# Queries on the un-normalized residual: five of sixteen query slabs of a product-key expert layer, and the row products beside them

## The chip, the cores and the metric

One core of one Trainium2 chip. The time is device microseconds of one execution of the whole program, from first to last instruction with what lies around them; several executions make a median. Lower is better.

The engines are PE (TensorE, matrix products; PEld is its weight load), DVE (VectorE), ACT (ScalarE), POOL (GpSimd) and SP, whose queue issues most DMAs. Each runs its own instructions in order and waits on semaphores for the others.

## The reference, cut to what matters

256 tokens of 1024 features pass through a first block (modulation, mixer, experts) and then two layers of a second block. The part in question is the seam between the mixer's output and the experts' queries:

```python
x = x + g1[:, None, :] * rms_norm(y, norm1_post[l])
h = modulate(rms_norm(x, norm2_pre[l]), sh2, sc2)      # h * (1 + sc2) + sh2
y = peer(h, peer_wq[l], ...)

def peer(h, wq, subkeys, u, v):
    q = (ht @ wq).reshape(T, P_HEADS, 2, P_DKH)         # 16 slabs of 128 columns
    s = jnp.einsum('thcd,hcnd->thcn', q, subkeys)       # scores, then top-k
    ...                                                 # experts u and v
```

The deviation of rms_norm is one number for each token. So with `A = norm2_pre * (1 + sc2)` and `B = sh2` for each feature and `r` for each token, `h @ wq = r * ((x * A) @ wq) + B @ wq`: `r` can go onto the product's result, and `B @ wq` is one number for each query column.

The second block's modulation is a matrix product of one row: `mod = silu(c2) @ mod_w + mod_b`, 6 x 1024 numbers for each of its layers. It needs nothing of the tokens, so it can be computed anywhere before its use.

## The kernel before, in words

All activations lie transposed: features on the 128 partitions, 8 chunks of 128 features by 256 tokens. A product in fp32 is three matmuls (`mm3`, L402-406): both operands are split into a rounded high half and the remainder, and high x high, high x low and low x high are added in PSUM. Weights come in slabs of 128 output columns (512 KB) into five raw buffers; `warm` (L308-325) splits a slab ahead of its use, the high half on ACT (L315), the low half on DVE (L323). `block` (L408) runs one slab: 8 chunks x 3 products. `blocks` (L424) runs several slabs chunk by chunk, so that each chunk of the input is used by all of them as soon as it is there. What follows a slab's products is a generator: `spawn` queues it, and `advance("pre")` and `advance("post")` in each later block take it one step further. The order of instructions on each engine is the order in which this Python code issues them; no scheduler changes it.

The seam before, in the order of issue (L1082-1159):

- w_out, 8 slabs. Each result is scaled into `y` (L1082) and squared on ACT; sums over tokens' features are products with a column of ones (`colstat`, L567).
- `resid_rms` (L660): the deviation (`rstd` L581: one DVE step, a power on POOL), its broadcast over the partitions by PE (`bcast2`, L576), then chunk by chunk `y` x deviation (L671), the residual's addition (L674), the square of the new `x` on ACT (L1104), the second norm's sums on PE.
- `peer` (L1129-1141): the second deviation and its broadcast, then `x` x deviation on DVE (L1137), `* A + B` on ACT (`affine`, L681), the high half on ACT (L683) and the low half on DVE (L400).
- The copy of `x` to memory (`xd`, L1145) and the load of the subkeys (`sub`, L1391), both issued by POOL.
- `blocks` of query slabs 0 to 2, then `block` for slabs 3 to 15. Each slab's result is copied by ACT (L1418), multiplied by the subkeys on PE (L1422), and sorted on DVE by a side generator (`topk`).

Both norms are chains on DVE, ACT and POOL. Beside them PE runs the class `Rows` (L227-265): the first 8 units of 128 columns of `mod`, as products of a single weight column with 512-column pieces of the weight's rows, 32 matmuls that show as 64 records. `PAUSES` says how many of them stand at which of the seam's places, and the rest stand behind the second broadcast (L1146). The result is a row, which ACT copies out of PSUM (L259) and POOL sends through memory to become columns (L261, L262).

The other units of `mod` are row dots on DVE (`dot`, L519-523), one unit for each 512 KB load and instruction of 128x1024 (L522). They are spread over other stages: `RATES[0]` is how many of them stand beside each block of the v stage (784 to 1140 us), from its sixth block to its 123rd.

Of the kernel before, what the change touches and what calls it, by code (L numbers as in the profile page):

```python
# [11 lines left out]
F32 = mybir.dt.float32  # L12
F32R = mybir.dt.float32r
# [15 lines left out]
RATES = [0.54, 0.0, 0.45, 0.4, 0.5, 0.15]  # L29
# [16 lines left out]
ROW_UNITS = 8  # L46
PAUSES = [3, 2, 2, 2, 2, 2, 2, 1, 0, 3, 3]
# [3 lines left out]
OFF, HALF = 4, 8  # L51
EPS = 1e-6
# [6 lines left out]
SPANS = (slice(0, 1), slice(1, 2), slice(2, 4), slice(4, 6), slice(6, 8))  # L59
# [70 lines left out]
def _rowsN(w):  # L130

    return np.ascontiguousarray(w.reshape(-1, P, w.shape[1]))
# [13 lines left out]
def _layout(i):  # L146
    o = {}
# [26 lines left out]
    o["mod0r"] = _rowsN(np.ascontiguousarray(i["mod_w_2"][0][:, :ROW_UNITS * P]))  # L174
# [7 lines left out]
    m = i["mla_w_in_2"][0]  # L182
# [4 lines left out]
    r = uq[:, :, 128:]  # L187
# [39 lines left out]
class Rows:  # L227


    def __init__(self, body, name, c8, place, depth):  # L230
        self.b, self.w, self.c8, self.place, self.depth = body, body.a[name], c8, place, depth
        self.raws, self.at, self.ps = [], 0, None
        self.load(depth)

    def load(self, n):
        while len(self.raws) < min(n, KC):
            raw = self.place()
            self.b.nc.sync.dma_start(raw, self.w[len(self.raws)])
            self.raws.append(raw)

    def step(self, n):

        if self.ps is None:
            self.ps = [self.b.pst() for _ in range(2)]
        for _ in range(min(n, 4 * KC - self.at)):
            kc, q = divmod(self.at, 4)
            self.b.nc.tensor.matmul(self.ps[q // 2][0:1, (q % 2) * T:(q % 2 + 1) * T], self.c8[:, kc:kc + 1],
                                    self.raws[kc][:, q * T:(q + 1) * T], start=kc == 0 and q % 2 == 0, stop=kc == KC - 1,
                                    skip_group_check=True)
            self.at += 1  # L250
            if q == 3:
                self.load(kc + 1 + self.depth)

    def finish(self, dst, bias, scr):

        nc = self.b.nc
        self.step(4 * KC)
        for n in range(2):
            nc.scalar.activation(scr[:, n * 512:(n + 1) * 512], self.ps[n][0:1], AF.Copy)  # L259
        line = self.b.dr.tile([1, D], F32, name="line")  # L260
        nc.gpsimd.dma_start(line, scr)  # L261
        nc.gpsimd.dma_start(dst, line.rearrange("o (k p) -> p (o k)", p=P))  # L262
        yield "post"
        yield "post"
        nc.vector.tensor_tensor(dst, dst, bias, ALU.add)


class Body:
# [391 lines left out]
    def resid_rms(self, st, y, dst, scr, then, idle=lambda n: None):  # L660

        nc = self.nc
        r = self.rstd(st, 2, EPS, D)
        self.warm()
        idle(0)
        bc = self.bcast2(r)
        for n in range(len(SPANS) + 1):
            idle(n + 1)
            if n < len(SPANS):
                s = SPANS[n]  # L670
                nc.vector.tensor_tensor(scr[:, s], y[:, s], self.wide(bc, s), ALU.mult)  # L671
            if n > 0:
                s = SPANS[n - 1]
                nc.vector.tensor_tensor(dst[:, s], scr[:, s], self.x[:, s], ALU.add)  # L674
                then(s)

# [44 lines left out]
    def mixer(self):  # L721
        nc, a = self.nc, self.a
        with ExitStack() as ctx:
            self.tmps = ctx.enter_context(self.pool_l("tmps1", 14))
            sp = ctx.enter_context(self.pool_l("mix", 1))
            self.mctx = ExitStack()
            mp = self.mctx.enter_context(self.pool_r("mraw", 4))
# [3 lines left out]
            x = self.x  # L731

            c8 = self.cp.tile([P, KC], F32, name="c8")
# [331 lines left out]
            self.prate = 0.0  # L1065
            c82 = self.cp.tile([P, KC], F32, name="c82")
            nc.scalar.activation(c82, self.colr("c2", 0, KC), AF.Sigmoid)
            nc.vector.tensor_tensor(c82, c82, self.colr("c2", 0, KC), ALU.mult)
            rows = self.rows = Rows(self, "mod0r", c82, lambda: mp.tile([P, D], F32, name="mraw"), 4)
# [23 lines left out]
            self.drain()  # L1093
            for j in range(8):
                if j == 7:
                    self.warm()
                self.block("w_out", j, mixa, g_y(j))
            self.drain()
            st2 = self.st2 = self.pst()

            wait = []

            def then(s):
                nc.scalar.activation(sgm[:, s], x[:, s], AF.Square)  # L1104
                if wait:
                    w = wait.pop()
                    nc.vector.tensor_tensor(sgm[:, w.start], sgm[:, w.start], sgm[:, w.start + 1], ALU.add)
                    self.colstat(st2, sgm[:, w.start], 0, False)
                if s.start in (2, 4):
                    wait.append(s)  # L1110
                else:
                    for j in range(s.start, s.stop):
                        self.colstat(st2, sgm[:, j], 0, j == 0)
            self.resid_rms(st, y, x, sga, then, lambda n: rows.step(PAUSES[1 + n]))


    def peer(self):
        tc, nc, a = self.tc, self.nc, self.a
        NB = 88
        with ExitStack() as ctx:  # L1120
# [8 lines left out]
            r = self.rstd(self.st2, 2, EPS, D)  # L1129
            self.rows.step(PAUSES[9])  # L1130
            bc = self.bcast2(r)
            self.rows.step(PAUSES[10])
            a2 = self.scale_cols("a2", self.colr("norm2_pre", 0, 8), self.ada[:, 32:40])
            self.warm()
            low = None
            for s in SPANS:
                nc.vector.tensor_tensor(za[:, s], self.x[:, s], self.wide(bc, s), ALU.mult)  # L1137
                if low:
                    low()
                low = self.affine(za, a2, self.ada[:, 24:32], h, s, za[:, 8 + s.start:10 + s.start])  # L1140
# [5 lines left out]
            self.rows.step(4 * KC)  # L1146
            self.mctx.close()
            self.xctx.close()
            tctx = ExitStack()
            tp = tctx.enter_context(self.pool_r("topk", 1))  # L1150
# [4 lines left out]
            self.blocks([("wq", b) for b in range(3)], h, [g_q(b) for b in range(3)], tail=3)  # L1155
            self.spawn(self.rows.finish(self.mod[0][:, 0:8], self.colr("mod_b", 0, 8), za[0:1, 20:24].rearrange("p a t -> p (a t)")))
            self.side, self.side_rate = side, 1.4
            for b in range(3, 16):
                self.block("wq", b, h, g_q(b))
# [227 lines left out]
    def topk(self, tp, t2, iota, iT, ss):  # L1387
# [27 lines left out]
        def g_q(b):  # L1415
            def gen(pq):
                q = t2.tile([P, T], F32, name="q")
                nc.scalar.activation(q, pq[:, :T], AF.Copy)  # L1418
# [664 lines left out]
```

## Time and profile before

| | |
|---|---|
| median of 3 runs | 1738.02 us (1731.5 to 1740.38) |
| profiled execution | 1743.28 us |
| its span | 1741.4 us |
| PE busy | 1707.6 us (98%) |
| DVE busy | 1382.3 us (79%) |
| ACT busy | 1038.1 us (60%) |
| POOL busy | 215.7 us (12%) |
| mean granted clock of PE | 0.992 |

The profile is of one execution, the times are of three others. Busy shares are means over stages. A row of a timeline gives the start, the duration, the engine, the line of the kernel, what is written and read, how many instructions the row holds, and in brackets how long the engine was idle before and what released it. PE's matmuls overlap: the distance of two starts, not the duration, is what one costs. [...]

### The profile page before, as it was taken

How to read it: one execution, taken by the hardware profiler on the slowest of the kernel's cores; microseconds unless marked ns; L12 is line 12 of the kernel's file. 1: busy time of each engine (PE TensorE's matmuls, PEld its weight loads, DVE VectorE, ACT ScalarE, POOL GpSimd, SP SyncE). 2: the span in 40 equal slices, each digit the busy share in tenths (PEclk: the TensorE clock that was granted, in tenths of full speed). 3: DMA queues.
4: the chain of work that ended last, by engine and by line, in shares of the span. 5: the costliest groups of instructions: out<-in, count | busy, mean ns of one | idle time of the engine just before them, and what ended most of it. 6: DMA issues, size and time to landing. Idle time of an engine off the chain costs nothing.

```text
span 1741.4 us, 33346 instructions
## 1 busy us (share of the span) xinstructions
PE 1707.6 (98%) x12720; PEld 1595.9 (92%) x12720; DVE 1382.3 (79%) x2845; ACT 1038.1 (60%) x1912; POOL 215.7 (12%) x236
## 2 busy tenths in 40 slices
PE   8999999999999999999999999999999999999997
PEld 4899999799999999998888888889999998999997
DVE  3788778679988889997888888876899867688754
ACT  3764444455554999985555555556675457567543
POOL 1110000000010775540000000030200000020001
PEclk8999999999999999999999999999999999999999
DMA  7676677545555454447898888853467665446552
GB/s 271 244 262 214 232 246 248 206 158 178 187 193 183 160 166 161 158 167 251 295 328 301 293 296 308 282 190 123 130 241 279 246 239 169 147 133 206 183 184 70
DMA packets 102400, 371.17 MB, mean 213 GB/s; under 512 B 11456, under 2 KB 11968, under 8 KB 101856
## 3 DMA queue, kind: packets, MB, share of 16 engines
q1 hardware_dynamic: 101664, 365.76, 61.8%
q0 software_dynamic: 576, 3.29, 0.5%
q8 instruction: 99, 1.62, 0.4%
q14 instruction: 61, 0.50, 0.1%
HBM read 365.99 MB, written 2.10 MB: 211 GB/s over the span
## 4 chain that ended last, share of the span: by engine, by line
PE 91%; DVE 4%; ACT 3%; issue 1%; POOL 1%; DMA 0%; POOLq 0%; ACTq 0%; DVEq 0%
PE ps L404 20%; PE ps L406 19%; PE ps L405 19%; PE ps L1282 6%; PE ps L1281 6%; PE ps L1283 6%; PE ps L1210 2%; PE ps L571 1%; PE ps L451 1%; PE ps L452 1%; PE ps L453 1%; PE ps L746 1%; PE ps L476 1%; PE ps L478 1%; PE ps L477 1%
## 5 line engine op out<-in xcount | busy, mean ns | idle before, releaser
L315 ACT ACTIVATE whi<-wraw 128x1024 fp32r<-128x1024 f32 (+1 forms) x548 | 573.8, 1050 | 447.2 <-PE ps L405 194.2
L323 DVE TENSOR_TENSOR wlo<-wraw,whi 128x1024 fp32r<-128x1024 f32 (+1 forms) x538 | 650.5, 1213 | 52.7 <-ACT whi L315 51.4
L404 PE MATMUL ps<-h2h,whi 128*128 128x256 f32 x1152 | 329.8, 286 | 0.0
L406 PE MATMUL ps<-h2h,wlo 128*128 128x256 f32 x1152 | 320.3, 278 | 0.6 <-DVE wlo L323 0.6
L405 PE MATMUL ps<-h2l,whi 128*128 128x256 f32 x1152 | 317.4, 276 | 0.0
L406 PE MATMUL ps<-hhh,wlo 128*128 128x256 f32 x800 | 225.2, 281 | 4.2 <-DVE wlo L323 4.2
L404 PE MATMUL ps<-hhh,whi 128*128 128x256 f32 x800 | 228.1, 285 | 0.8 <-ACT hhh L683 0.8
L405 PE MATMUL ps<-hhl,whi 128*128 128x256 f32 x800 | 224.9, 281 | 1.3 <-DVE hhl L400 1.1
L404 PEld LDWEIGHTS ps<-h2h,whi 128*128 128x128 f32 x1152 | 216.4, 188 | 0.4 <-ACT za L681 0.4
L405 PEld LDWEIGHTS ps<-h2l,whi 128*128 128x128 f32 x1152 | 216.7, 188 | 0.0
L406 PEld LDWEIGHTS ps<-h2h,wlo 128*128 128x128 f32 x1152 | 215.5, 187 | 0.9 <-DVE wlo L323 0.8
L1282 PE MATMUL ps<-whi,al 128*128 128x512 f32 x512 | 199.5, 390 | 0.8 <-DVE al L400 0.8
L1281 PE MATMUL ps<-whi,ah 128*128 128x512 f32 x512 | 199.2, 389 | 0.0
L1283 PE MATMUL ps<-wlo,ah 128*128 128x512 f32 x512 | 199.2, 389 | 0.0
L1202 POOL TENSOR_SCALAR L<-iota,i1T,eT 128x128 bf16<-128x128 f32 x128 | 141.0, 1108 | 272.3 <-DVE mT L1504 137.0
L522 DVE SCALAR_TENSOR_TENSOR mraw<-mraw,crow 128x1024 f32<-128x1024 f32 x128 | 157.2, 1228 | 0.0
L406 PEld LDWEIGHTS ps<-hhh,wlo 128*128 128x128 f32 x800 | 150.9, 189 | 4.8 <-DVE wlo L323 4.8
L404 PEld LDWEIGHTS ps<-hhh,whi 128*128 128x128 f32 x800 | 152.1, 190 | 2.4 <-ACT hhh L683 1.6
L405 PEld LDWEIGHTS ps<-hhl,whi 128*128 128x128 f32 x800 | 151.2, 189 | 2.7 <-DVE hhl L400 2.4
L404 PE MATMUL ps<-hh,whi 128*128 128x256 f32 (+1 forms) x440 | 126.0, 286 | 0.7 <-ACT hh L683 0.7
L406 PE MATMUL ps<-hh,wlo 128*128 128x256 f32 (+1 forms) x440 | 123.2, 280 | 0.5 <-DVE wlo L323 0.5
L405 PE MATMUL ps<-hl,whi 128*128 128x256 f32 (+1 forms) x440 | 122.9, 279 | 0.2 <-DVE hl L400 0.2
(463 smaller groups left out, 3511.4 us busy)
## 6 DMA issues: line engine op xcount, KB each, us to landing
wraw<-u SPq DMA_DIRECT2D x128, 512.0 KB, 3.3
wraw<-v SPq DMA_DIRECT2D x128, 512.0 KB, 5.4
mraw<-mod SPq DMA_DIRECT2D x88, 512.0 KB, 3.9
wraw<-fa SPq DMA_DIRECT2D x44, 512.0 KB, 4.2
wraw<-fb SPq DMA_DIRECT2D x44, 512.0 KB, 4.1
mraw<-w_ada SPq DMA_DIRECT2D x40, 512.0 KB, 4.2
wraw<-fo SPq DMA_DIRECT2D x32, 512.0 KB, 4.4
wraw<-wq SPq DMA_DIRECT2D x16, 512.0 KB, 3.8
```

Source lines behind the costliest of these rows:

```text
L315: nc.scalar.activation(t[:, :hi - lo], self.raws[self.n_hi][:, :hi - lo], AF.Copy)
L323: e.tensor_tensor(t[:, :n], self.raws[self.n_lo][:, :n], self.his[self.n_lo].bitcast(F32)[:, :n], ALU.subtract)
L404: mm(out, lh, rh, start=start, stop=False, **kw)
L405: mm(out, lh, rl, start=False, stop=False, **kw)
L406: mm(out, ll, rh, start=False, stop=stop, **kw)
L451: mm(pts[tt][hf], ah, wh[:, s], start=kc == 0, stop=False)
L522: nc.vector.scalar_tensor_tensor(raw, raw, 1.0, self.crow, op0=ALU.mult, op1=ALU.mult, accum_out=acc)
L1202: nc.gpsimd.tensor_scalar(L[:, k], iota, i1, e, op0=ALU.is_equal, op1=ALU.mult)
L1210: nc.tensor.matmul(pg[:, k * P:(k + 1) * P], L[:, k], half[:, k, h], start=h == 1, stop=h == 0)
L1281: mm(o, ah, w[0][:, s], start=first, stop=False)
L1282: mm(o, al, w[0][:, s], start=False, stop=False)
L1283: mm(o, ah, w[1][:, s], start=False, stop=last)
```

## The change: what it does

- The residual's chunks go into query products without the second deviation. For each chunk, ACT makes the high half of `x * A` (`pre`), DVE the low half, and PE multiplies it with slabs 0, 1 and 2 at once (`prods`), beside the sums of squares. Two further columns of `pre` hold `B`, so that each product has 258 columns and the last two give `B @ wq`.
- Slabs 3 and 4 follow on the same `pre`. Behind the third chunk of slab 3 stands the second broadcast. For slabs 3 and 4 the split weights lie in spare buffers (`w4h`, `w4l`) over a tile that is free by then.
- Then `h2` is made from `x` for slabs 5 to 15: ACT copies the broadcast to SBUF (`br`), and for each chunk DVE computes `x * A * br`, ACT adds `B` and rounds, DVE makes the low half. Between the chunks stand the splits of the weights of slabs 5 to 7.
- The results of slabs 0 to 4 (`g_ql`): DVE copies the two last columns, multiplies by `br`, ACT adds `B @ wq`; then the subkeys' products as before. The side generator of the sort starts four slabs later.
- The additions of pairs of squares move from DVE to POOL. `A` and `B` are prepared during the mixer's products rather than between the norms.
- `ROW_UNITS` is 4 rather than 8: 16 row matmuls rather than 32, from two loads of 1 MB rather than eight of 512 KB. 4 of them stand before the first norm's sums, 12 between the sums and the first broadcast. The other four units become row dots on DVE: 132 rather than 128. `RATES[0]` goes from 0.54 to 0.58.

The core of the diff:

```diff
-RATES = [0.54, 0.0, 0.45, 0.4, 0.5, 0.15]
+RATES = [0.58, 0.0, 0.45, 0.4, 0.5, 0.15]
...
-ROW_UNITS = 8
-PAUSES = [3, 2, 2, 2, 2, 2, 2, 1, 0, 3, 3]
+ROW_UNITS = 4
+PAUSES = [4, 12]
...
             self.drain()
-            st2 = self.st2 = self.pst()
-
+            r = self.rstd(st, 2, EPS, D)
+            self.warm(5, 5)
+            rows.step(PAUSES[1])
+            self.spawn(rows.finish(self.mod[0][:, 0:4], self.colr("mod_b", 0, 4)))
+            self.advance("post")
+            bc = self.bcast2(r)
+            ws = [self.use(("wq", b, 0, D)) for b in range(3)]
...
+            def prods(k, b):
+                s = slice(k * P, (k + 1) * P)
+                self.mm3(qs[b][:, :T + 2], ws[b][0][:, s], ws[b][1][:, s], pre[0][:, k], pre[1][:, k], k == 0, k == KC - 1)
+
+            def high(s):
+                js = range(s.start, s.stop)
+                square = lambda: nc.scalar.activation(sgm[:, s], x[:, s], AF.Square)
+                if s.stop == KC:
+                    square()
+                for j in js:
+                    nc.scalar.activation(pre[0][:, j, :T], x[:, j], AF.Copy, scale=a2[:, j:j + 1])
+                if s.stop < KC:
+                    square()
+
+            def low(s):
+                js = range(s.start, s.stop)
+                for j in js:
+                    nc.vector.scalar_tensor_tensor(pre[1][:, j, :T], x[:, j], a2[:, j:j + 1], pre[0].bitcast(F32)[:, j, :T],
+                                                   op0=ALU.mult, op1=ALU.subtract)
                 if wait:
                     w = wait.pop()
-                    nc.vector.tensor_tensor(sgm[:, w.start], sgm[:, w.start], sgm[:, w.start + 1], ALU.add)
+                    nc.gpsimd.tensor_tensor(sgm[:, w.start], sgm[:, w.start], sgm[:, w.start + 1], ALU.add)
...
+                for j in js:
+                    for b in range(3):
+                        prods(j, b)
...
+            r = self.rstd(st2, 2, EPS, D)
+            self.warm(4, -9)
+            for b in (3, 4):
+                ws.append(self.use(("wq", b, 0, D)))
+                qs.append(self.pst())
+                for k in range(KC):
+                    prods(k, b)
+                    if b == 3 and k == 2:
+                        self.br = self.bcast2(r)
...
-            for s in SPANS:
-                nc.vector.tensor_tensor(za[:, s], self.x[:, s], self.wide(bc, s), ALU.mult)
+            for j in range(KC):
+                t = self.tmp("nx")
+                nc.vector.scalar_tensor_tensor(t, self.x[:, j], a2[:, j:j + 1], br, op0=ALU.mult, op1=ALU.mult)
+                nc.scalar.activation(h[0][:, j], t, AF.Identity, bias=b2[:, j:j + 1])
                 if low:
                     low()
...
+                if j in (1, 3, 5):
+                    self.warm(1 + j // 2, 1 + j // 2)
             low()
...
+            def g_ql(b):
+
+                pt = self.lead_q[b]
+                w = self.sm.tile([P, 2], F32, name="wq")
+                nc.vector.tensor_copy(w, pt[:, T:T + 2])
+                q = qlp.tile([P, T], F32, name="ql")
+                nc.vector.tensor_tensor(q, pt[:, :T], br, ALU.mult)
+                nc.scalar.activation(q, q, AF.Identity, bias=w[:, 0:1])
+                for _ in range(b // 2):
+                    yield "pre"
+                yield from g_q(b, q)(None)
+            for b in range(5):
+                self.spawn(g_ql(b))
+            self.advance("post")
+            self.blocks([("wq", b) for b in (5, 6)], h, [g_q(b) for b in (5, 6)])
```

How the order of instructions moves, at three places. First PE between w_out and the first query products. In the kernel before, where L247 is a row product, L571 a sum with the column of ones, L576 a broadcast, `mxh` w_out's input and `sgm` the squares:

```order
L406 MATMUL ps<-mxh,wlo 128x256
L247 MATMUL ps<-mraw,c_3186 1x256 x3
L571 MATMUL ps<-ones,ysum 128x1 x2
L571 MATMUL ps<-ones,t_ysq 128x1 x2
L247 MATMUL ps<-mraw,c_3186 1x256 x2
L576 MATMUL ps<-ident,rr 128x128 x2
L247 MATMUL ps<-mraw,c_3186 1x256 x4
L571 MATMUL ps<-ones,sgm 128x1 x2
```

From there on row products stand between all the sums, and the last 13 of them between the second broadcast and the first product of `h2h`. In the changed kernel (L244 the row product, L566 the sum, L571 the broadcast, `prqh` and `prql` the halves of `pre`, `rwhm` and `rwvs` the two 1 MB loads):

```order
L401 MATMUL ps<-mxh,wlo 128x256
L244 MATMUL ps<-rwhm,c_3190 1x256 x4
L566 MATMUL ps<-ones,ysum 128x1 x2
L566 MATMUL ps<-ones,t_ysq 128x1 x2
L244 MATMUL ps<-rwhm,c_3190 1x256 x4
L244 MATMUL ps<-rwvs,c_3190 1x256 x8
L571 MATMUL ps<-ident,rr 128x128 x2
L566 MATMUL ps<-ones,sgm 128x1 x2
L399 MATMUL ps<-prqh,whi 128x258
L400 MATMUL ps<-prql,whi 128x258
L401 MATMUL ps<-prqh,wlo 128x258
```

All row products stand ahead of the first broadcast, and query products follow behind the first sum of the new squares.

Second, PE at the end of slab 4 in the changed kernel (`sub` the subkeys, `ql` a query of `g_ql`, `h2h` and `h2l` the halves of h2):

```order
L401 MATMUL ps<-prqh,w4l 128x258
L1474 MATMUL ps<-sub,ql 128x128 x4
L399 MATMUL ps<-h2h,whi 128x256
L400 MATMUL ps<-h2l,whi 128x256
L401 MATMUL ps<-h2h,wlo 128x256
```

The subkey products of slabs 0 and 1 stand ahead of the first product on h2.

Third, DVE behind the second deviation. In the kernel before:

```order
L588 TENSOR_SCALAR rv<-ps 128x2
L648 SCALAR_TENSOR_TENSOR a_3874<-ada,cols 128x8
L1137 TENSOR_TENSOR za<-x,ps 128x256 x2
L400 TENSOR_TENSOR h2l<-za,h2h 128x256
L1137 TENSOR_TENSOR za<-x,ps 128x512
```

In the changed kernel, the end of the h2 chunks (L318 is the weight split, L1171 `x * A * br`, L1175 the low half) and the first result of `g_ql`:

```order
L318 TENSOR_TENSOR wlo<-wraw,whi 128x1024
L1171 SCALAR_TENSOR_TENSOR t_nx<-x,a_3197,i1T 128x256
L1175 SCALAR_TENSOR_TENSOR h2l<-t_nx,ada,h2h 128x256
L1171 SCALAR_TENSOR_TENSOR t_nx<-x,a_3197,i1T 128x256
L1175 SCALAR_TENSOR_TENSOR h2l<-t_nx,ada,h2h 128x256 x2
L1197 COPY wq<-ps 128x2
L1199 TENSOR_TENSOR ql<-ps,i1T 128x256
```

Each chunk of h2 takes two instructions of DVE with 256 columns, and the results of slabs 0 to 4 are taken up only behind the last chunk.

## Rows read from the trace of the kernel before

**Rows 1.** page, part 4: chain that ended last, by engine

```profile
PE 91%; DVE 4%; ACT 3%; issue 1%; POOL 1%; DMA 0%; POOLq 0%; ACTq 0%; DVEq 0%
```

**Rows 2.** windows: stretch, us, each engine's busy us (instructions), PEclk, DMA share, GB/s

```profile
322.00:344.00 22.00, 21.91 (x120) 11.46 (x119) 13.75 (x30) 10.12 (x20) 4.00 (x37) 1.00 0.59 204
```

**Rows 3.** PE's timeline, 318 to 368 us: start, us, instructions, [idle before, releaser]

```profile
322.74 0.28 PE L406 MATMUL ps<-mxh,wlo 128*128 128x256 f32 x1
...
326.59 0.71 PE L576 MATMUL ps<-ident,rr 128*128 128x128 f32 x4
...
337.41 5.77 PE L247 MATMUL ps<-mraw,c 128*1 128x256 f32 x26
343.11 0.39 PE L404 MATMUL ps<-h2h,whi 128*128 128x256 f32 x1
...
351.70 0.28 PE L404 MATMUL ps<-h2h,whi 128*128 128x256 f32 x1
...
354.69 1.85 PE L1422 MATMUL ps<-sub,q 128*128 128x128 f32 x12
...
367.05 0.38 PE L406 MATMUL ps<-h2h,wlo 128*128 128x256 f32 x1 [0.60 <-DVE wlo L323]
```

**Rows 4.** VectorE's timeline, 322 to 362 us

```profile
327.34 0.75 DVE L671 TENSOR_TENSOR sga<-y,ps 128x256 f32<-128x256 f32 x2 [0.23 <-PE ps L576]
328.01 0.42 DVE L674 TENSOR_TENSOR x<-sga,x 128x256 f32<-128x256 f32 x1
...
350.75 3.50 DVE L323 TENSOR_TENSOR wlo<-wraw,whi 128x1024 fp32r<-128x1024 f32 x3 [4.80 <-ACT whi L315]
```

**Rows 5.** ScalarE's timeline, 322 to 362 us

```profile
328.46 0.42 ACT L1104 ACTIVATE sgm<-x 128x256 f32<-128x256 f32 x1 [2.61 <-DVE x L674]
...
349.66 3.18 ACT L315 ACTIVATE whi<-wraw 128x1024 fp32r<-128x1024 f32 x3 [4.44 <-PE ps L405]
```

**Rows 6.** POOL's timeline, 322 to 362 us

```profile
336.58 0.76 POOL L1145 DMA_DIRECT2D xd<-x  x1
```

**Rows 7.** timeline of all engines, 1226 to 1230 us, VectorE and POOL

```profile
1227.08 0.74 POOL L1733 TENSOR_TENSOR t_zp<-z 128x256 f32<-128x256 f32 x1 [54.60 <-DVE z L1617]
1227.12 0.98 DVE L1625 SCALAR_TENSOR_TENSOR prel<-z,lnAB,preh 128x256 fp32r<-128x256 f32 x1 [0.19 <-ACT preh L1622]
...
1228.02 0.47 DVE L1617 SCALAR_TENSOR_TENSOR z<-ps,mod,x 128x256 f32<-128x256 f32 x1
...
1228.42 0.47 DVE L1625 SCALAR_TENSOR_TENSOR prel<-z,lnAB,preh 128x256 fp32r<-128x256 f32 x1
```

**Rows 8.** DMA issues, 300 to 365 us: KB each, median us to landing

```profile
xd<-x POOLq DMA_DIRECT2D x1, 1024.0 KB, 9.3
sub<-subk POOLq DMA_DIRECT2D x1, 1024.0 KB, 10.9
```

**Rows 9.** PE's timeline and windows around two gaps of 1.70 us

```profile
1569.19 0.39 PE L406 MATMUL ps<-hhh,wlo 128*128 128x256 f32 x1 [1.70 <-DVE wlo L323]
...
1570.03 0.42 PE L406 MATMUL ps<-hhh,wlo 128*128 128x256 f32 x1
...
1573.24 0.35 PE L406 MATMUL ps<-hhh,wlo 128*128 128x256 f32 x1
...
1571.00:1572.00 1.00, 1.00 (x7) 1.00 (x7) 1.00 (x2) 1.00 (x2) 0.00 (x0) 0.50 0.83 324
...
1267.48 0.38 PE L406 MATMUL ps<-hhh,wlo 128*128 128x256 f32 x1 [1.70 <-DVE wlo L323]
...
1268.00:1272.00 4.00, 4.00 (x36) 4.00 (x36) 3.94 (x8) 3.50 (x7) 0.00 (x0) 1.00 0.61 186
```

**Rows 10.** v stage: a window, waits for v, group of row dots

```profile
960.00:1050.00 90.00, 90.00 (x398) 74.47 (x398) 79.02 (x141) 51.28 (x79) 0.00 (x0) 1.00 0.87 297
...
ACT whi L315 <- DMA wraw<-v: 3.8, 2, 2.2
...
L522 DVE SCALAR_TENSOR_TENSOR mraw<-mraw,crow 128x1024 f32<-128x1024 f32 x128 | 157.2, 1228 | 0.0
```

More of the change, by code (lines that the diff above doesn't have):

```diff
@@ L227, with __init__ @@
 class Rows:
[L230 to L239, printed above, removed]
+    def __init__(self, body, name, c8, raws):
+        self.b, self.c8, self.raws = body, c8, raws
+        self.at, self.ps = 0, None
+        for n, raw in enumerate(raws):
+            body.nc.sync.dma_start(raw, body.a[name][n])
@@ L241, in step @@
     def step(self, n):
         if self.ps is None:
[L244 to L249, printed above, removed]
+            self.ps = self.b.pst()
@@ L250, in step, with finish @@
+        for _ in range(min(n, 2 * KC - self.at)):
+            kc, q = divmod(self.at, 2)
+            o = (kc % 4) * 2 * T + q * T
+            self.b.nc.tensor.matmul(self.ps[0:1, q * T:(q + 1) * T], self.c8[:, kc:kc + 1], self.raws[kc // 4][:, o:o + T],
+                                    start=self.at == 0, stop=kc == KC - 1, skip_group_check=True)
             self.at += 1
-            if q == 3:
-                self.load(kc + 1 + self.depth)
-    def finish(self, dst, bias, scr):
+    def finish(self, dst, bias):
@@ L262, in finish @@
         nc.gpsimd.dma_start(dst, line.rearrange("o (k p) -> p (o k)", p=P))
-        yield "post"
-        yield "post"
+        for _ in range(3):
+            yield "post"
         nc.vector.tensor_tensor(dst, dst, bias, ALU.add)
@@ L658, in wide @@
         return ap.unsqueeze(1).broadcast_to([P, s.stop - s.start, T])
[L660 to L675, printed above, removed]
     def affine(self, x, A, B, act, s, scr):
@@ L1068, in mixer @@
             nc.vector.tensor_tensor(c82, c82, self.colr("c2", 0, KC), ALU.mult)
-            rows = self.rows = Rows(self, "mod0r", c82, lambda: mp.tile([P, D], F32, name="mraw"), 4)
+            rows = Rows(self, "mod0r", c82, [sp.tile([P, 2 * D], F32, name="rw" + t, tag=t) for t in ("hm", "vs")])
+            a2 = self.a2 = self.scale_cols("a2", self.colr("norm2_pre", 0, 8), self.ada[:, 32:40])
+            pre = tuple(qp.tile([P, KC, T + 16], F32R, name="prq" + m)[:, :, o:o + T + 2] for m, o in (("h", 12), ("l", 4)))
+            b2 = self.cp.tile([P, KC, 2], F32, name="b2")
+            for n in range(2):
+                nc.vector.tensor_copy(b2[:, :, n], self.ada[:, 24:32])
+            self.split(b2, pre[0][:, :, T:], pre[1][:, :, T:])
             for j in range(8):
@@ L1093, in mixer @@
             self.drain()
+            pair = [sp.tile([P, 2 * D + HALF], F32R, name="w4" + m, tag="ya" + m)[:, :2 * D].rearrange("p (a t) -> p a t", t=D) for m in "hl"]
             for j in range(8):
@@ L1111, in then @@
                 else:
-                    for j in range(s.start, s.stop):
+                    for j in js:
                         self.colstat(st2, sgm[:, j], 0, j == 0)
-            self.resid_rms(st, y, x, sga, then, lambda n: rows.step(PAUSES[1 + n]))
+                for j in js:
+                    for b in range(3):
+                        prods(j, b)
+            for n in range(len(SPANS) + 2):
+                if n < len(SPANS):
+                    s = SPANS[n]
+                    nc.vector.tensor_tensor(sga[:, s], y[:, s], self.wide(bc, s), ALU.mult)
+                if 0 < n <= len(SPANS):
+                    s = SPANS[n - 1]
+                    nc.vector.tensor_tensor(x[:, s], sga[:, s], x[:, s], ALU.add)
+                    high(s)
+                if n > 1:
+                    low(SPANS[n - 2])
+            r = self.rstd(st2, 2, EPS, D)
[7 more added lines that the diff above has]
+                        self.br = self.bcast2(r)
     def peer(self):
@@ L1145, in peer @@
             nc.gpsimd.dma_start(xd, self.x)
-            self.rows.step(4 * KC)
-            self.mctx.close()
+            self.qctx.close()
             self.xctx.close()
             tctx = ExitStack()
+            qlp = tctx.enter_context(self.pool_r("ql", 5))
             tp = tctx.enter_context(self.pool_r("topk", 1))
@@ L1154, in peer @@
             g_q = next(side)
-            self.blocks([("wq", b) for b in range(3)], h, [g_q(b) for b in range(3)], tail=3)
-            self.spawn(self.rows.finish(self.mod[0][:, 0:8], self.colr("mod_b", 0, 8), za[0:1, 20:24].rearrange("p a t -> p (a t)")))
+            def g_ql(b):
[12 more added lines that the diff above has]
+            self.blocks([("wq", b) for b in (5, 6)], h, [g_q(b) for b in (5, 6)])
             self.side, self.side_rate = side, 1.4
-            for b in range(3, 16):
+            for b in range(7, 16):
                 self.block("wq", b, h, g_q(b))
@@ L1413, in top16, with g_q, gen @@
                 nc.vector.tensor_copy(idx, u)
[L1415 to L1418, printed above, removed]
+        def g_q(b, q=None):
+            def gen(pq, q=q):
+                if q is None:
+                    q = t2.tile([P, T], F32, name="q")
+                    nc.scalar.activation(q, pq[:, :T], AF.Copy)
                 yield "pre"
```

33 lines of the change are left out of this document (19 added, 14 removed).

## The prediction

> **What bounds the kernel now.** I read the chain that ended last first: 91% of the span is PE [rows 1]. So a change of this kernel is worth what it takes from, or adds to, PE's own stream of instructions, idle time included. Second the stretch that the change rewrites, 322 to 344 us: PE is busy 21.91 of 22.00 us there at a granted clock of 1.00 [rows 2]. The reader should see that this is a full engine and not a free one: VectorE and ScalarE have room there (13.75 and 10.12 us busy), PE none. Third PE's timeline, to see with what it is full [rows 3]: between w_out's last product (322.74) and the first query product (343.11) it does almost nothing but row products, the last 26 of which start at 337.41 and fill the 5.70 us in which h2 is made. They are useful work that covers two norms one behind the other. So the question is what covers the norms when half of that work is gone.
>
> **What is taken away.** Row products fall from 64 records to 32. One costs 5.70/26 = 0.22 us [rows 3], so PE loses 32 x 0.22 = **7.0 us** of work. That is the whole gain: every other matmul stays (the query products grow from 256 to 258 columns, 1%, for 120 of them some 0.1 us, left out).
>
> **Gap a, before the first query product.** Four row steps (8 records, 1.8 us) and the four pairs of norm sums end at about 325.9, as before. Twelve steps (24 records x 0.22 = 5.3 us) carry PE to 331.2; under them lie the norm's small operations and the splitting of three slabs, three ScalarE passes of 3.18 together and three VectorE passes of 3.50 together [rows 4, 5]. Then the broadcast of the deviation ends at 331.9, and PE has nothing more. The chain behind it, from rows of the same operations: the first y x deviation starts 0.75 after the broadcast does (327.34 against 326.59 [rows 3, 4]); two of them and the residual add take 328.01 + 0.42 - 327.34 = 1.1 [rows 4]; ScalarE's high half, then its square, 0.42 each, 0.84 [rows 5]. 331.2 + 0.75 + 1.1 + 0.84 = 333.9. PE idles **2.0 us**. Longer if the semaphores between the engines add up, shorter by nothing that I can see, since the first square is what the first sum on PE waits for.
>
> **The three slabs on the residual.** 72 products at (351.70 - 343.11)/72 = 0.119 us [rows 3] are 8.6 us, the sums 3.3; VectorE's chunks come faster than PE takes them (a 128x256 step of the kind (a x scalar) - b has starts 0.40 apart [rows 7]), once the first two are through. I put 0.4 us of waiting on that start-up. The two additions that go to POOL have a price on VectorE: beside POOL's 0.74 us addition the same step took 0.98 rather than 0.47 [rows 7]. Twice 0.5 us falls where VectorE is ahead of PE, so the sum takes 0, bound 1.0. [...]
>
> **Gap b, before the first subkey product.** This is the term that decides. PE goes on with 9 products of slab 3 and the second broadcast, whose result ScalarE copies to SBUF by about 348.4 (333.9 + 8.6 + 3.3 + 0.4 = 346.2; 1.1 for nine products, 0.7 broadcast, 0.4 copy). Only then does VectorE begin to make h2, chunk by chunk: 16 steps at 0.39 us = 6.3, two weight splits in between at 1.17 = 2.3 [rows 4], a wait of about 1.2 for the high half of the last of these slabs (ScalarE takes 1.06 for one [rows 5], behind its own h2 chunk), 0.6 for two waits on ScalarE: 10.4 us, to 358.8. Behind all of it, on the same engine, stand the copy and the multiplication for the first of the five slabs (0.4); ScalarE's bias is 0.5 more; PE's next instruction is the product of that query with the subkeys, at 359.7. The order of PE has these in front of the products of slabs 5 and 6, which would have h2 chunks to work on from 349 on. PE itself is through with slab 4 at 346.2 + 48 x 0.119 + 0.6 = 352.5. Idle: **7.2 us**. Bounds: 0.335 us a step, the distance of the plain two-operand steps at 327.34 [rows 4], and no wait for the high half would leave 5.1; a price of 0.47 each, with no overlap, makes 8.5. I keep 7.2, since the trace has the same form of step at 0.40.
>
> **Small terms.** The wait of PE at 367.05 for a weight split, 0.60 [rows 3], goes: -0.6, because that slab (7) is split under gap b. The subkeys' transfer is issued behind the copy of x on POOL's queue, 0.76 us after it [rows 6]; both wait for nothing but the second deviation and go out at about 345.2 and 345.9; 10.9 us [rows 8] later, at 356.8, the subkeys have landed, 2.9 us before they are wanted. Nothing is charged; what it is if they are late, stands among the rivals. Four more 128-wide units of mod become VectorE's row dots, 1.23 us each [rows 10], and their 512 KB loads, in the v stage with 118 blocks x 0.04 = 5 pieces more than now. There VectorE is busy 79.02 of 90 us and PE 90.00 [rows 10]: 5 x 1.5 us vanish in VectorE's idle time as long as the loads behave.
>
> **The clock.** PE's granted clock was 1.00 all through this stretch because PE never stopped. Twice the trace has a gap of 1.70 us before a product. [...] A stay at the lower level: from 1570.03 to 1573.24 PE started 15 products in 3.21 us, at 0.119 each 1.79 would have done, so a drop costs 1.4 us [rows 9]. Gap b is four times longer than one that was followed by a drop, gap a a little longer: I charge both, 2 x 1.4 = **2.8 us**. [...]
>
> **The sum.** -7.0 + 2.0 + 0.4 + 7.2 - 0.6 + 2.8 = **+4.8 us**. Against the profiled execution, 1743.28, that is 1748.1; the median of the runs shown is 1738.02, 5.3 below the profiled one, and the forecast is made against it: **1742.8 us**. 0.5%, about what a measurement of this kernel can tell from no change, is 8.7 us, so the likeliest outcome is no difference that counts. The gain cannot pass 7.0 + 0.6 = 7.6 us even with both gaps gone.
>
> **Rivals.**
> - *Shorter gaps.* VectorE's steps come 0.335 apart (16 x 0.055 = 0.9), the high half is there in time (1.2), and gap a leaves the clock alone (1.4): 4.8 - 3.5 = +1.3, **1739.3**. For it: the gap of 1.70 without a drop, and ScalarE's idle time before the last split. Against: the 0.40 of [rows 7].
> - *The v stage loses its cover* (the other side). The five further 512 KB pieces come into a stretch whose DMA share is 0.87 at 297 GB/s [rows 10]. If the v slabs, which have to land in time for ScalarE's split, are pushed back by them, PE waits: 5 x 512 KB at 297 GB/s is 8.8 us, +13.6 in all, **1751.6**. It decides from the point at which the landing takes longer than the buffers hold; ScalarE waited for v slabs twice already, 3.8 us in all [rows 10], which speaks for it. Against: PE was busy 90.00 of 90 us there in spite of that.
> - *The subkeys land late.* If the copy of x (9.3) and the subkeys (10.9) [rows 8] run one behind the other and not side by side, the subkeys land at 345.9 + 20.2 = 366.1, 6.4 after the query wants them: +11.2, **1749.2**. In the kernel before nothing shows it, as the subkeys had 17 us there.
> - *The change does not do what it says*, so that PE's stream is as before: excluded, as the order of instructions shows 16 row matmuls rather than 32 and the products on the residual ahead of h2.
>
> **How the numbers follow.** Forecast 0.72, shorter gaps 0.18, v stage 0.05, subkeys 0.05. From the forecast (+4.8) another 3.9 us makes it slower by over 0.5%, which the bounds of gap b (+1.3) and the POOL additions (+1.0) with the spread of medians reach in a small part: 0.05; faster by over 0.5% needs 13.5 us, a measurement's accident: 0.02; same 0.65. Shorter gaps: same 0.16, faster 0.02. The v stage: slower 0.04, same 0.01; the subkeys the same. Together: **faster 0.04, same 0.83, slower 0.13**. The range goes from the shorter gaps less the distance of the lowest run to the median (1739.3 - 6.5 = 1733) to the v stage's price, 1752.
>
> **What would show it.** In the changed kernel's profile: 32 row records, PE idle about 2 us before the first sum of squares and about 7 us before the first subkey product, that one released by ScalarE's bias; granted clock 0.50 for some 3 us after each; no wait of PE in slab 7; the v stage as long as before. Wrong if the gap before the subkeys is under 4 us or ends with a DMA, if the clock stays at 1.00 behind both, or if the v stage is longer by more than 2 us.

## The result, and the profile of the changed kernel

The changed kernel takes 1757.68 us (median of 6 runs, 1754.27 to 1762.07) beside 1739.55 us of the kernel before on the same chip: ratio 1.0096, 95% interval 1.007 to 1.0121. A second measurement on another occasion gave 1.0093 (1.0076 to 1.0109). By these ratios it is slower by 16 to 17 us. The forecast was 1742.8 us and no difference that counts, with a range that ended at 1752: the change costs time that counts, and the measured time lies outside the range.

The two gaps of the seam came out as forecast. PE's timeline of the changed kernel, from the row products to the first subkey product; these rows answer to [rows 3]:

```profile
320.17 1.89 PE L244 MATMUL ps<-rwhm,c 128*1 128x256 f32 x8
...
324.69 3.62 PE L244 MATMUL ps<-rwvs,c 128*1 128x256 f32 x16
328.24 0.71 PE L571 MATMUL ps<-ident,rr 128*128 128x128 f32 x4
330.97 0.61 PE L566 MATMUL ps<-ones,sgm 128*128 128x1 f32 x4 [2.02 <-ACT sgm L1107]
...
345.00 0.60 PE L571 MATMUL ps<-ident,rr 128*128 128x128 f32 x4
...
357.56 2.08 PE L1474 MATMUL ps<-sub,ql 128*128 128x128 f32 x8 [7.28 <-ACT ql L1200]
```

The two gaps are 2.02 and 7.28 us, the second is released by ScalarE's bias, and the row products cost 0.22 us a record (16 in 3.55 us). Two windows behind the gaps, with the granted clock in the third column from the end:

```profile
334.00:336.00 2.00, 2.00 (x11) 2.00 (x11) 2.00 (x5) 1.50 (x4) 1.29 (x2) 0.50 0.04 1
...
358.00:360.00 2.00, 2.00 (x11) 2.00 (x11) 0.92 (x5) 1.42 (x3) 0.00 (x0) 0.50 0.05 12
```

Behind both gaps the granted clock was 0.50 (the prediction's lower level), and so it was in a second profile of the changed kernel, where products started 0.21 us apart behind each. That the first gap brought it is not shown. In a second profile of the kernel before, which has no such gap, the granted clock was 0.50 at the same place, while PE was busy throughout with the row products and a broadcast:

```profile
333.30:336.60 3.30, 3.30 (x10) 1.38 (x9) 0.64 (x2) 0.12 (x1) 2.96 (x36) 0.50 1.01 287
```

With the gap of 2.0 us the granted clock was 0.50 there in all seven profiles, without it in two of the five that have the order of the kernel before.

What the forecast had no term for is seen in the v stage. A window of it, which answers to the first row of [rows 10], and the three groups of its products:

```profile
961.40:1051.40 90.00, 90.00 (x389) 72.96 (x388) 79.78 (x145) 49.31 (x75) 0.00 (x0) 1.00 0.87 300
```

```profile
L1333 PE MATMUL ps<-whi,al 128*128 128x512 f32 x512 | 202.4, 395 | 0.8 <-DVE al L395 0.8
L1332 PE MATMUL ps<-whi,ah 128*128 128x512 f32 x512 | 202.0, 395 | 0.0
L1334 PE MATMUL ps<-wlo,ah 128*128 128x512 f32 x512 | 202.0, 394 | 0.0
```

PE is busy 90.00 of 90 us as before, the clock is 1.00 as before, it waits for nothing, and yet it did 389 products where the kernel before did 398. The mean distance of two starts over the stage, waits left out, is 0.2324 us rather than 0.2267: 1536 products x 0.0057 = 8.7 us. Busy share, waits and granted clock all look untouched; only the count in a window of fixed length tells.

Stage by stage, in us, each from the start of a kind of product to the start of the next, of two profiles of each kernel (the second ones from the runs below):

| stage | before | before, again | changed | changed, again |
|---|---|---|---|---|
| start to w_out's last product | 322.7 | 320.0 | 320.0 | 322.5 |
| to the last subkey product | 76.4 | 78.6 | 79.6 | 82.6 |
| to the first one-hot product | 170.3 | 170.3 | 171.3 | 171.3 |
| to the v stage | 217.2 | 217.2 | 217.2 | 217.2 |
| v stage, to its last product | 349.6 | 349.5 | 358.3 | 360.4 |
| to the span's end | 605.2 | 605.8 | 606.1 | 604.7 |

On the means: seam (the second row) +3.6, the stage behind it +1.0, v stage +9.8, the rest -0.2. That is 14.2 of the 16 to 17 measured, inside the interval. Most of the seam's spread within one kernel goes with the clock. PE worked 3.4 us at a granted clock of 0.50 there in the second profile of the kernel before and none in the first; 6.5 and 13.0 us in the two of the changed kernel.

### The profile page after: what moved, and what is told of

Read it like the earlier page. It is cut to its first block, busy times and chain, and to the rows that moved or that the text cites. A ratio compares the mean times of both kernels' runs of the same rounds, so it can differ in the third digit from the quotient of the medians.

```text
span 1752.5 us, 33329 instructions
## 1 busy us (share of the span) xinstructions
PE 1710.2 (98%) x12688; PEld 1596.8 (91%) x12688; DVE 1394.7 (80%) x2882; ACT 1039.3 (59%) x1917; POOL 224.3 (13%) x239
## 4 chain that ended last, share of the span: by engine, by line
PE 85%; DVE 8%; ACT 4%; issue 2%; DMA 1%; POOL 0%; ACTq 0%; DVEq 0%; SPq 0%; POOLq 0%
PE ps L399 19%; PE ps L401 19%; PE ps L400 19%; PE ps L1333 5%; PE ps L1334 5%; PE ps L1332 5%; DVE wlo L318 2%; PE ps L1261 2%; DVE mraw L517 1%; PE ps L566 1%; PE ps L724 1%; PE ps L471 1%; PE ps L473 1%; PE ps L472 1%; DMA wraw<-v 1%
## 5 line engine op out<-in xcount | busy, mean ns | idle before, releaser
L310 ACT ACTIVATE whi<-wraw 128x1024 fp32r<-128x1024 f32 x546 | 571.5, 1050 | 447.3 <-PE ps L400 181.4
L318 DVE TENSOR_TENSOR wlo<-wraw,whi 128x1024 fp32r<-128x1024 f32 (+1 forms) x536 | 648.0, 1213 | 55.9 <-ACT whi L310 54.5
L399 PE MATMUL ps<-h2h,whi 128*128 128x256 f32 x1112 | 318.6, 287 | 0.0
L401 PE MATMUL ps<-h2h,wlo 128*128 128x256 f32 x1112 | 309.7, 279 | 0.0
L400 PE MATMUL ps<-h2l,whi 128*128 128x256 f32 x1112 | 307.3, 276 | 0.0
L399 PEld LDWEIGHTS ps<-h2h,whi 128*128 128x128 f32 x1112 | 209.6, 188 | 0.0
L400 PEld LDWEIGHTS ps<-h2l,whi 128*128 128x128 f32 x1112 | 209.5, 188 | 0.0
L401 PEld LDWEIGHTS ps<-h2h,wlo 128*128 128x128 f32 x1112 | 208.4, 187 | 0.0
L1253 POOL TENSOR_SCALAR L<-iota,i1T,eT 128x128 bf16<-128x128 f32 x128 | 146.1, 1148 | 284.2 <-PE ps L401 160.5
L517 DVE SCALAR_TENSOR_TENSOR mraw<-mraw,crow 128x1024 f32<-128x1024 f32 x132 | 161.9, 1227 | 0.2 <-DMA mraw<-mod 0.2
```

The costliest lines, as they stand in the source:

```text
L310: nc.scalar.activation(t[:, :hi - lo], self.raws[self.n_hi][:, :hi - lo], AF.Copy)
L318: e.tensor_tensor(t[:, :n], self.raws[self.n_lo][:, :n], self.his[self.n_lo].bitcast(F32)[:, :n], ALU.subtract)
L399: mm(out, lh, rh, start=start, stop=False, **kw)
L400: mm(out, lh, rl, start=False, stop=False, **kw)
L401: mm(out, ll, rh, start=False, stop=stop, **kw)
L517: nc.vector.scalar_tensor_tensor(raw, raw, 1.0, self.crow, op0=ALU.mult, op1=ALU.mult, accum_out=acc)
```

## Experiments

**Theory 1**: the slower products come from placement. The change has two new small tiles in the pools that lie first in SBUF (`b2`, 64 bytes a partition; `wq`, 2 x 32). They lift the weights' raw buffers and halves by 128 bytes (the first `whi` from 41664 to 41792), while the v stage's small operand (`ah` at 184256), in a pool that the kernel puts on the right side, stays. The distance of the two was a multiple of 256 bytes (184256 - 41664 = 142592 = 557 x 256) and is 128 off it now. **Theory 2**: the five further row dots and their loads in the v stage slow PE down, my rival of the v stage.

### The kernel before, lifted by 128 bytes

```diff
         cp = self.cp
+        cp.tile([P, 32], F32, name="shift")
```

> The kernel before with one unused tile of 128 bytes a partition in the pool that lies first in SBUF; nothing else is changed. In the changed kernel two small new tiles (64 bytes each) move the weights' halves, their raw buffers and all that lies behind them on the left side up by 128 bytes, while the activations of the v stage on the right side stay where they were. Theory 1 (placement): PE's products in the v stage read two operands whose distance decides their rate. Then this kernel has the v stage of the changed kernel: starts of products 0.2324 us apart rather than 0.227, the stage 358 us rather than 349.4, and the time 7 to 12 us above the kernel before. Theory 2 (the five further pieces and their loads slow PE down in the v stage): v stage 349.4 us, time within 3 us of the kernel before.

Measured: ratio 1.0052 (1.0031 to 1.0072), v stage 359.1 us, 0.2333 us a product. 128 unused bytes cost the kernel before about 9 us by the ratio (7.3 between the medians). Its window, with 388 products:

```profile
960.00:1050.00 90.00, 90.00 (x388) 72.39 (x387) 77.05 (x136) 50.11 (x76) 0.00 (x0) 1.00 0.84 289
```

### The changed kernel with its small tiles on the other side

```diff
-            b2 = self.cp.tile([P, KC, 2], F32, name="b2")
+            b2 = qp.tile([P, KC, 2], F32, name="b2")
...
-                w = self.sm.tile([P, 2], F32, name="wq")
+                w = qlp.tile([P, 2], F32, name="wq")
```

> The changed kernel with its two small new tiles on the right side of SBUF, so that the weights and all else on the left lie at the addresses of the kernel before. Theory 1 (placement): v stage 349.4 us, 0.227 us a product, and 8 to 9 us less than the changed kernel, which leaves the +4.8 us of the prediction's sum against the kernel before, of which 3 to 4 are seen between w_out's end and the first expert slab. Theory 2 (pieces): v stage 358 us, time as the changed kernel's.

Measured: ratio to the kernel before 1.0045 (1.002 to 1.0069), so 1749.87 us beside 1742.34; 0.2269 us a product, v stage 351.7 us. What is left, +7.5 us, is the seam (80.9 us, +2.3 to +4.4), 2.8 in the stage behind it, and 2.2 in the v stage, most of it waiting (below).

```profile
960.00:1050.00 90.00, 90.00 (x398) 74.16 (x396) 81.69 (x148) 50.36 (x76) 0.00 (x0) 1.00 0.89 304
```

This window holds more row dots than the window of [rows 10] and PE does its 398 products.

### The changed kernel with the old rate of row dots

```diff
-RATES = [0.58, 0.0, 0.45, 0.4, 0.5, 0.15]
+RATES = [0.54, 0.0, 0.45, 0.4, 0.5, 0.15]
```

> The changed kernel with RATES[0] at 0.54 again, so that the v stage has as many row dots and loads as before; the others are done later. Theory 1 (placement): v stage 358 us and 0.2324 us a product as in the changed kernel. Theory 2 (pieces): v stage 349.4 us, 0.227 us a product.

Measured in one profile: v stage 357.8 us, 0.2324 us a product. Theory 2 falls as the cause of the slower products. The first five blocks of the stage, which have no row dots beside them yet, are slow in the changed kernel as well: 0.2322 against 0.2275.

### Distance or address

The changed kernel with its weights left where they are, and the small operand lowered instead:

```diff
                     asplit(0)
+                    vp2.tile([P, 16], F32, name="shift")
```

> The changed kernel with the weights where it has them (128 bytes higher than in the kernel before) and the v stage's small operand (ah, al) lowered by 128 bytes, by an unused tile of 2 x 64 bytes in its pool, so that the distance of the two is that of the kernel before plus 256 bytes. If the distance of the two operands modulo 256 bytes sets the rate: 0.227 us a product, v stage 350 to 352 us. If the weights' own address does: 0.2324, 358 us.

Measured in one profile: 0.2268 us a product. With both operands moved the rate is that of the kernel before (0.2267); with one of them moved it was 0.2324 and 0.2333. So in this stage the distance of PE's two operands counts, not where either lies. (The raw buffers lie at a fixed distance from the halves in all these versions, so no run tells whether the small operand meets the halves that PE reads or the buffers and halves that the other engines read and write meanwhile.) The v stage took 354.9 us all the same, because of one wait near its end, with a granted clock of 0.50 for 3.4 us behind it. The wait shows what the five further pieces really cost. VectorE's and PE's timelines:

```profile
1135.94 1.22 DVE L517 SCALAR_TENSOR_TENSOR mraw<-mraw,crow 128x1024 f32<-128x1024 f32 x1 [3.08 <-DMA mraw<-mod]
...
1137.28 1.23 DVE L318 TENSOR_TENSOR wlo<-wraw,whi 128x1024 fp32r<-128x1024 f32 x1
1138.43 0.42 DVE L395 TENSOR_TENSOR al<-zb,ah 128x256 fp32r<-128x256 f32 x1
```

```profile
1138.90 0.72 PE L1334 MATMUL ps<-whi,al 128*128 128x512 f32 x1 [3.45 <-DVE al L395]
```

The last row dot of the stage waits 3.08 us for its load, the weight split and the small operand's low half stand behind it on VectorE, and PE waits 3.45 us for that. So the rival of the v stage is there, with 1.7 to 3.5 us of PE's time in the versions with fast products and the rate of 0.58 (1.70 with the small tiles on the other side), through the pieces' own load and not the v slabs'. In the changed kernel, whose products are slower, VectorE waits 0.2 us for a piece in the first profile and PE 0.32 us near the stage's end, where the kernel before waits 0.18.

The kernel before, lifted by 64 bytes:

```diff
         cp = self.cp
+        cp.tile([P, 16], F32, name="shift")
```

> The kernel before with an unused tile of 64 bytes rather than 128 in front, so that the distance is 64 bytes off a multiple of 256. If the rate falls with the distance from a multiple of 256: products 0.227 to 0.2333 us apart, most likely between. If only 128 matters: 0.227, v stage 349.6.

Measured in one profile: 0.2289 us a product, v stage 353.0 us. Between the two, as the first reading had it.

Sixteen distances in one kernel:

```diff
-                ah = vp2.tile([P, T], F32R, name="ah")
-                al = vp2.tile([P, T], F32R, name="al")
+                o = 4 * (i2 // 8)
+                ah = vp2.tile([P, T + 64], F32R, name="ah")[:, o:o + T]
+                al = vp2.tile([P, T + 64], F32R, name="al")[:, o:o + T]
```

> The kernel before with the v stage's small operand (ah, al) in tiles 256 bytes longer, in which it starts 16 bytes further every eight blocks of the 128: 0 bytes from a multiple of 256 to the weights' halves in blocks 0 to 7, 16 in blocks 8 to 15, and so on to 240. So one profile holds sixteen distances. If the distance modulo 256 bytes sets the rate of the products, the distance of their starts is 0.227 us in the first eight blocks, 0.229 in those at 64 (blocks 32 to 39) and 0.232 to 0.233 in those at 128 (blocks 64 to 71), as in the kernels that were shifted as a whole; if it is an address alone, all sixteen are alike at 0.227. Nothing is expected of the others; one below 0.2267 would be worth using.

Measured in one profile. The mean distance of consecutive starts in each stretch of eight blocks (some 90 products each; each pair of neighbouring records in the timeline, those over 0.3 us left out):

```
bytes   0      16     32     48     64     80     96     112
us      0.2275 0.2331 0.2333 0.2333 0.2332 0.2319 0.2343 0.2332
bytes   128    144    160    176    192    208    224    240
us      0.2333 0.2333 0.2333 0.2301 0.2289 0.2332 0.2333 0.2272
```

So twelve of the sixteen distances have the slow rate, 0.2319 to 0.2343 us. The fast one stands at a multiple of 256 bytes (0.2275) and 16 below it (240: 0.2272), with values between at 176 (0.2301) and 192 (0.2289); the 0.2275 at 0 is also what the kernel before has in its first eight blocks (0.2274). My guess of a rate that falls with the distance is wrong: 16 bytes (0.2331) are as bad as 128 (0.2333). The kernel lifted by 64 bytes has the distance 192 in this table and its very rate, 0.2289; the one lifted by 128 has 0.2333, as here. The kernel before lay on one of the two best places.

### The kernel before once more

Its edit is none.

> The kernel before, unchanged, for a second profile of it. If the stages outside the seam and the v stage differ between kernels by what they do (170.4 us between the last subkey product and the first one-hot product before, 171 to 173 after), it has 170.4 again; if they differ from execution to execution, it lies anywhere from 170 to 173. The v stage should be 349.6 within 0.5.

Measured: 170.3 us in the stage behind the seam, v stage 349.5 us. In the first profile they were 170.3 and 349.6. The seam, though, had 78.6 us rather than 76.4: PE's wait in slab 7 was 1.25 us rather than 0.60, and the granted clock was 0.50 for 3.4 us (the line in the section on the result), with no gap ahead of it.

### The second gap: the order of PE, or its data

In the version with the small tiles on the other side, where `take` is what `g_ql` did first (copy, multiplication, bias), for slab 0 into a tile that is free by then:

```diff
...
+            take(0)
             low = None
             for j in range(KC):
                 t = self.tmp("nx")
...
             def g_ql(b):
...
-                for _ in range(b // 2):
+                if b:
+                    take(b)
+                for _ in range(b // 2 + 1):
                     yield "pre"
```

> The changed kernel with both small tiles placed as in the run before it, the first of the five results taken up ahead of the h2 chunks (0.43 us on VectorE; it frees the PSUM bank of slab 6), and the subkey products of slabs 0 to 4 one block later, so that slabs 5 and 6 stand in front of them. If the second gap is what the prediction says, a wait of PE's order and not of its data, PE works through slabs 5 and 6 at the pace of the h2 chunks (about 1.3 us a chunk) and is through with slab 6 about 5 us earlier than the changed kernel: the idle time of 7.3 us in one piece goes, some 2 us in pieces are left, and the time is 13 to 15 us below the changed kernel (8.7 of them placement), 0 to 2 us below the kernel before. If something else holds the first subkey product and h2 (the subkeys' landing, the clock), the gain over the run before it is under 2 us.

Measured: 1744.40 us beside 1742.34, ratio 1.0004 (0.999 to 1.0018), 5.5 us below the run with only the tiles moved. Against the kernel before it is level by the ratio, where 0 to 2 us less was expected. The seam takes 73.6 us rather than 80.9; the v stage gives 1.4 of that back (353.1 us, a wait of 1.91 us near its end). The longest idle time of PE left there and the window's clock:

```profile
356.17 0.39 PE L400 MATMUL ps<-h2l,whi 128*128 128x256 f32 x1 [1.45 <-DVE h2l L1184]
```

```profile
352.00:358.00 6.00, 4.50 (x36) 4.07 (x35) 4.69 (x13) 2.81 (x5) 0.00 (x0) 1.00 0.54 173
```

The 7.28 us were PE's order: with slabs 5 and 6 in front, and their data no earlier, 1.5 us of idle time in six are left, and a clock of 1.00.

### Two versions that go further

First the old rate again, and the high half of slab 7 early, its low half behind the h2 chunks:

```diff
-RATES = [0.58, 0.0, 0.45, 0.4, 0.5, 0.15]
+RATES = [0.54, 0.0, 0.45, 0.4, 0.5, 0.15]
...
-                if j in (1, 3, 5):
-                    self.warm(1 + j // 2, 1 + j // 2)
+                if j in (1, 3):
+                    self.warm(2 + j // 2, 1 + j // 2)
             low()
+            self.warm(3, 3)
```

> The late subkey products of the run before, and further: RATES[0] at 0.54, which should take away the wait of 1.9 us near the v stage's end (PE for VectorE's low half, VectorE behind with row dots); and the weight split of slab 7 behind the h2 chunks rather than among them, its high half early, which takes 2.3 us out of VectorE's chain. If both count as the profile shows them, it is 3 to 4 us below the late subkey products (1744.4 beside 1742.3), 1 to 2 us below the kernel before. If the slack is taken up elsewhere (the sort, which starts four slabs late), no gain over that run.

Measured: 1741.04 beside 1740.76, ratio 1.0003 (0.9989 to 1.0017): no gain that can be told from the version before. The seam has 73.9 us, as before; the wait at the v stage's end is down to 0.18 us, but the stage still takes 351.5, with a wait of 0.93 for ScalarE's high half elsewhere in it.

Then 4 of the 12 row steps behind the first broadcast, on top of it:

```diff
+        yield "post"
         nc.gpsimd.dma_start(dst, line.rearrange("o (k p) -> p (o k)", p=P))
...
-            rows.step(PAUSES[1])
-            self.spawn(rows.finish(self.mod[0][:, 0:4], self.colr("mod_b", 0, 4)))
-            self.advance("post")
+            rows.step(8)
             bc = self.bcast2(r)
+            rows.step(4)
...
             r = self.rstd(st2, 2, EPS, D)
+            self.spawn(rows.finish(self.mod[0][:, 0:4], self.colr("mod_b", 0, 4)))
+            self.advance("post")
```

> The version with the late subkey products, RATES[0] at 0.54 and the early high half of slab 7, and now 4 of the 12 row steps behind the first broadcast rather than ahead of it (the row's way through memory is issued later, behind the subkeys' load). 8 records at 0.22 us then cover 1.8 of the 2.0 us of the first gap, and the broadcast starts 1.8 us earlier: -1.8 us, and -1.4 if the clock then stays at 1.00. Expected 2 to 3 us below that version (1741.0 beside 1740.8). If VectorE's weight splits, which stand ahead of the first multiplication, hold it as before, the gap stays and nothing is gained.

Measured: 1736.43 us beside 1739.92, ratio 0.9978 (0.9964 to 0.9992), 3.5 us below the kernel before and the only version here that beats it. The first gap is 0.21 us, and the clock stays at 1.00 behind it:

```profile
324.71 0.71 PE L572 MATMUL ps<-ident,rr 128*128 128x128 f32 x4
325.35 1.89 PE L244 MATMUL ps<-rwvs,c 128*1 128x256 f32 x8
327.45 0.61 PE L567 MATMUL ps<-ones,sgm 128*128 128x1 f32 x4 [0.21 <-ACT sgm L1107]
```

The seam takes 69.6 us, 7 to 9 below the kernel before; the stage behind it gives 2.8 back (173.1 against 170.3).

### The changed kernel once more

> The changed kernel, unchanged, on the same chip as the version above. If the placement (8.7 us in the v stage) and the seam (3 to 5 us) are all there is, its ratio to the kernel before is 1.007 to 1.008 and the v stage 358.3 us again; the 1.0096 measured first would then hold 3 to 4 us that the chip or the runs put there. If something else costs time that the one profile did not catch, the ratio is 1.0096 again or above.

Measured: ratio 1.0093 (1.0076 to 1.0109), v stage 360.4 us (0.2324 us a product, the rest two waits of 1.19 and 0.80 us), seam 82.6. The first ratio holds, and no further stage shows up.

## Why the prediction was wrong, point by point

- *Row products, -7.0*: right, 32 records at 0.22 us.
- *Gap a, 2.0*: right, 2.02; 2.02 or 2.03 in the six others with the same order.
- *Gap b, 7.2*: right, 7.27 or 7.28 in five profiles, released by ScalarE's bias. Its parts were met too: VectorE's steps start 0.40 us apart, and its wait for the last high half is 1.12. That it is a matter of PE's order was shown by the late subkey products.
- *The clock, 2.8*: both gaps were followed by 0.50, but the cost varies. At 0.50 the products of 258 columns start 0.215 us apart in the changed kernel, at 1.00 they start 0.120 apart, so by estimate 44% of PE's time at 0.50 is lost: 2.9 us in the first profile (6.5 us there) and 5.7 in the second (13.0). The reason given for the 1.00 before, that PE never stopped, does not hold: in the second profile of the kernel before it never stopped either (busy 3.30 of 3.30 us), and the clock was 0.50 at the same place. So the charge for gap a is not shown to be the gap's.
- *The sum for the seam, +4.8*: +3.6 on the means of two profiles each, +4.5 on all five with the order of the kernel before (77.1 us) and all five with the changed order (81.6).
- *The subkeys' landing*: never the last thing that was waited for; that rival is out.
- *What is taken away*: here stands the step that failed, "every other matmul stays". The matmuls stay, their price does not: 1536 products of the v stage went from 0.2267 to 0.2324 us, 8.7 us, because the change's two small tiles moved one operand by 128 bytes against the other. I costed the edit that holds them (prepare `A` and `B` early, copy two columns) at nothing, and looked at its instructions only, not at what lies behind them in memory. The prediction named the sign that came, a v stage longer by more than 2 us, but no reason for it that holds.
- *The v stage as a rival*: its place and even its price (8.8 us) were met, by luck. Its mechanism, loads that push the v slabs back, was refuted by the old rate of row dots, with which the stage took 357.8 us. A small form of it exists, 1.7 to 3.5 us, where the last piece's own load is late.
- *No rival for it*: nothing in the profile of before showed that a rate could depend on an address, but the memory plan could have been compared beside the order of instructions, and shows the shift.

Open: the stage behind the seam is 1.0 us longer in the changed kernel and up to 2.9 in the versions with the tiles on the other side (170.3, 171.3, 173.1). PE does not wait there; its products start 0.1156 us apart in the kernel before over most of 400 to 550 us and 0.1178 throughout in those versions, at equal distances of their operands. In the changed kernel they go from 0.1156 to 0.1178 at some 490 us, and so they do in the version of the kernel before with sixteen distances (171.4 us), whose edit touches nothing but the v stage's small operand. So the 1.0 us is not shown to be the change's, and no run here tells why it is there. Of the 16 to 17 us, 2 to 3 are in no stage of the profiles and lie within the interval.

## What to carry to other kernels

Before costing a change, compare where the tiles lie, not only which instructions run: two new tiles of 64 bytes moved all that lies behind them against the tiles on the right side, and the v stage's products took 8.7 us more. When a stage gets longer with no wait, no clock and no instruction to show for it, count the products in windows of equal length. And work that stands in line for a late result does not belong ahead of work whose data is there: moving the subkey products behind two slabs of query products was worth 5.5 us.

## What the runs showed of the hardware that was not expected

In the v stage, where a 128x128 operand is loaded for each product (398 loads and 398 products in the window of [rows 10]) and 512 columns of another are multiplied, the distance of two starts was 0.2267 us with the operands' addresses a multiple of 256 bytes apart, 0.2272 at 240 above one, 0.2289 at 192, 0.2301 at 176, and 0.232 to 0.234 at the twelve other multiples of 16. The granted clock was 1.00 and PE busy 90.00 of 90 us in the windows of the kernels with one distance, 18.83 to 20.00 of 20 us in those of the version with sixteen. The rate followed the distance when the one operand was moved (the kernel before, lifted by 128 bytes: 0.2333) and came back when the other was moved after it (the changed kernel, its small operand lowered: 0.2268). Why, no run shows. POOL was busy 0.00 us in these windows, so no instruction of POOL slowed PE there.
